# A hybrid decoder block: weights split a block ahead, dense banks kept open, recurrence inputs moved

## The chip, the cores and the metric

The kernel runs on one core of one Trainium2 chip. The metric is device time in microseconds, the median of three runs. The core has a matrix engine (TensorE, PE in the profile; PEld is its weight load), and three engines for elementwise work: VectorE (DVE), ScalarE (ACT) and GpSimd (POOL). SyncE (SP) issues the DMAs of the weights. TensorE writes to PSUM, which has eight banks of 128 partitions by 512 float32 numbers; all other data lie in SBUF.

## The reference

One decoder layer over 512 positions of width 1024. The input is normalized and projected once (`xn @ w_in`), and the columns of the result go to four branches of width 512 and to their gates:

- A, forgetting attention, 8 heads of 64 with a cumulative log-sigmoid bias: `s = q.k * scale + c_i - c_k`, causal softmax, `o = p v`;
- B, a recurrence: a causal convolution of width 4 over `xb`, two sigmoid gates by block-diagonal matrices, then `h_t = a_t h_(t-1) + b_t`;
- C, sparse attention, 8 heads over 2 key heads, the gated sum of three attentions: over compressed blocks of 32 positions (a small MLP over 32 x 64 values with stride 16), over selected blocks (all of them here) and over a window;
- D, spatial gating: `gelu(ud)` times a causal mix of the layer-normed `gelu(vd)`.

Each branch is multiplied by the SiLU of its gate (`ga`, `gb`, `gc`, `gd`), projected to 1024 columns, weighted by `sigmoid(mg)` and summed; `out = x + merged @ w_out`.

## The kernel before

Every product is made from three float32r matmuls: each operand is split into a rounded high part and the rest, and high x high, low x high and high x low are summed in PSUM. So each weight block of 128 x 1024 is loaded (`load`, a 512 KB DMA into one of four `raw` buffers), cast to its high part on POOL or ACT (`hi_cast`) and subtracted on DVE (`wsplit`, three `w` buffers).

The projections are written as generators. `zgen` makes one bank (128 columns of the result, transposed, by 512 positions) in 8 steps of three matmuls of 512 columns. `nat` makes four banks (512 positions by 512 columns) from four weight blocks in 32 steps. A list `queue` holds such generators, and `fill(us)` runs steps from it, at an assumed `G` = 0.68 us a step, between the parts of an attention. `drain` empties it. These generators ask for the weight block when their turn comes, and `nat` takes its four banks at its start.

The attentions go by units, one head of one kind each. `scores` makes four score tiles (L503, L504), their masked maximum (L506, DVE) and exponential (L508, ACT), and calls `fill` after each. POOL scales the probabilities (L516). `finish` transposes them in pieces of 128 x 256 (L527), splits each piece (ACT L532, DVE L533), multiplies by the values (L540, L541), and calls `fill` between. `attend` runs `scores` of a unit ahead of `finish` of the one before.

The program order is:

1. `ka`, `qa`, `va` and the norm of x.
2. Attention A, 8 units, with a queue of `kv`, `qc`, `cm` (the inputs of the compression) and `vd`. Then `drain`, and `psum_banks` closes all PSUM pools and opens others.
3. Attention C, 16 units. `compress()` writes shifted copies of `cm` (`t2`, `trs`, L701 to L707), splits them (`tbl`, L709, L712), and runs the MLP (`hps`, L723) and makes the compressed keys `kc`. It runs beside the `ga` blocks (`both`), and the second unit waits for it in the program (`while not ready`). `ud`, `gd` and two blocks of `gc` are queued behind. Then `drain`, and `psum_banks` again.
4. The late stage: `xb` blocks, whose use copies each bank to SBUF (L960) and convolves it on DVE (L962, L966), the rest of `gc`, the gates (L979 to L983), gelus, the recurrence's scan, `gb`, and the first merge of branch A (`merge_plain`: `mg` blocks, then `project`). Then the spatial mix and the sums that the next stage needs.
5. Three merges by seven block products each (`seven`, `project`), and the output projection.

The program order is not the engines' order. The framework's planner simulates the program when it is built: it gives each engine the earliest written instruction that is ready by its own estimates, so that later work moves into gaps, as far as buffers and banks are free. A pool's memory that follows a closed pool is free when the old tiles have been read. Each engine then runs its list in that order, waiting where an operand is late.

Of the kernel before, what the change touches and what calls it, by code (L numbers as in the profile page):

```python
# [1 line left out]

# [58 lines left out]
def f32(ap):  # L61
    return ap.bitcast(F32)
# [3 lines left out]
def tile_hybrid_layer(ctx: ExitStack, tc: tile.TileContext, x, xT, units, small, bsp, out):  # L66
# [10 lines left out]
    def psum_banks(nz, nt, rest):  # L77

        if "stack" in ps_:
            ps_["stack"].close()  # L80
        ps_["stack"] = st = ExitStack()
        ps_["n"] += 1
        ps_.pop("m", None)
        ps_["nz"] = nz
        for nm in ("z", *rest):
            ps_[nm] = pool(f"{nm}p{ps_['n']}", st, space=PSUM)
        ps_["tb"] = [ps_["t"].tile([P, S], F32, name=f"tb{i}") for i in range(nt)] if nt else []
        ps_["ti"] = 0
# [4 lines left out]
    def four(name):  # L93

        if "m" in ps_:
            return [zbank(name + "0")] + [ps_["m"].tile([P, S], F32, tag="m", bufs=3, name=f"{name}{t}") for t in (1, 2, 3)]
        return [zbank(f"{name}{t}") for t in range(4)]
# [10 lines left out]
    psum_banks(4, 1, "sto")  # L108
# [61 lines left out]
    G = 0.68  # L170
    last = {}

    def zgen(key, b, use):

        hi, lo = wsplit(key, b)
        ps = zbank(f"z_{key}{b}")
        for k in range(KD):
            ks = slice(k * P, (k + 1) * P)
            PE.matmul(ps, lhsT=hi[:, ks], rhs=xh[:, k, :], start=k == 0, stop=False)  # L179
            PE.matmul(ps, lhsT=hi[:, ks], rhs=xl[:, k, :], start=False, stop=False)  # L180
            PE.matmul(ps, lhsT=lo[:, ks], rhs=xh[:, k, :], start=False, stop=k == KD - 1)  # L181
            if k == KD - 1:
                use(ps)
            yield G

    def nat(key, lhs_h, lhs_l, emit, fetch=None):

        banks = four(f"z_{key}")
        for c in range(4):
            hi, lo = (fetch or wsplit)(f"{key}.{c // 2}", c % 2)  # L190
            for t in range(4):
# [11 lines left out]
    queue, owed = [], [0.0]  # L203

    def fill(us):

        owed[0] += us
        while owed[0] > 0 and queue:
            c = next(queue[0], None)
            if c is None:  # L210
                queue.pop(0)
            else:
                owed[0] -= c
        owed[0] = min(owed[0], 0.0)

    def drain():
        while queue:
            fill(1.0)

    def both(a, b):  # L220

        live = [a, b]
        while live:
            c = 0.0
            for g_ in list(live):
                d = next(g_, None)
                if d is None:
                    live.remove(g_)
                else:
                    c += d  # L230
            if c:
                yield c
# [11 lines left out]
    def run(gen, n=10 ** 6):  # L244
        for _ in range(n):
            if next(gen, None) is None:
                return

# [193 lines left out]

    att = ExitStack()
# [158 lines left out]
    def cm_use(b):  # L602
        return lambda ps: ACT.copy(zcm[b], ps)
# [13 lines left out]
    for e, o in ((0, 64), (1, 0)):  # L617
        POOL.tensor_scalar(kts[1][1][o:o + 40, e, :], f32(nb), 1.0, 0.0, op0=ALU.mult, op1=ALU.add)
    queue += [nat("kv", xh, xl, emit_kv), nat("qc", xh, xl, emit_z(zq_c, ssc, 4, 8, ap)),
              zgen("cm0", 0, cm_use(0)), zgen("cm0", 1, cm_use(1)), nat("vd", xh, xl, emit_vd)]  # L620

    def fox_units():
        for i in range(4):
# [14 lines left out]
    def attend(units):  # L638
        prev = None
        for u in units:  # L640
            scores(u, G)
            if prev:
                finish(prev, GAPS)
            prev = u
        fill(6 * G)
        finish(prev, GAPS)

    attend(fox_units())
    drain()
    r1.close()  # L650
    psum_banks(3, 2, "sto")

    dp_ = pool("dp_", side="right")
    def tile8(name, dtype=F32):
        return dp_.tile([P, 4, S], dtype, tag="t8", bufs=2, name=name)

    r2 = ExitStack()
    rp2 = pool("rp2", r2, side="right")
# [15 lines left out]
    def silu(key, dst, blocks=(0, 1, 2, 3), keep=False):  # L674
        for i in blocks:
            yield from zgen(f"{key}{i // 2}", i % 2, silu_use(dst, i, key, keep))
# [10 lines left out]
    def compress():  # L687
# [7 lines left out]
        trs = rp2.tile([P, 2048], F32, name="trs")  # L695

        def prepare(n, nm):
# [3 lines left out]
            POOL.memset(tr[:, :, :, 31:32], 0.0)  # L701
            for g in range(2):
                t2 = ap.tile([P, S], F32, tag="ft", bufs=3, name=f"t2{nm}{g}")
                ACT.copy(t2[0:64, :], zcm[n][HALF[g], :])
                ACT.copy(t2[64:128, 0:511], zcm[n][HALF[g], 1:512])
                src = bass.AP(tensor=t2.tensor, offset=t2.offset, ap=[list(t2.ap[0]), [2, 16], [16, 31]])
                DVE.tensor_tensor(tr[:, :, g, 0:31], src, cc[:, POS:POS + 16].unsqueeze(2).to_broadcast([P, 16, 31]),  # L707
                                  op=ALU.add)
# [8 lines left out]
        def hidden(nm):  # L717
            hps = zbank("hps" + nm)[:, 0:256]
            for h in range(2):
                w = wsplit("w1" + nm, h, True)  # L720
# [39 lines left out]
        for c in prepare(1, "v"):  # L760
            yield c + next(gk)
# [82 lines left out]
    def gd_():  # L844
        sgd["t"] = ylp.tile([P, 4, S], F32, tag="z8", bufs=1, name="sgd")
        yield from silu("gd", sgd["t"], keep=True)

    queue.append(gd_())
# [3 lines left out]
    fill(4 * G)  # L852

# [34 lines left out]
    attend(nsa_units())  # L888
# [52 lines left out]
    psum_banks(3, 0, "mg")  # L941
# [15 lines left out]
    def xb_use(i):  # L957
        def use(ps):
            xb = lp.tile([P, S], F32, tag="xb", bufs=2, name=f"xb{i}")
            ACT.copy(xb, ps)  # L960
            xc[i] = ft(f"xc{i}", "xc", 4)
            DVE.tensor_scalar(xc[i], xb, cc[:, CONVW + 12 + i:CONVW + 13 + i], cc[:, CONVB + i:CONVB + i + 1],  # L962
                              op0=ALU.mult, op1=ALU.add)
            for k in (2, 1, 0):
                n = 3 - k
                DVE.scalar_tensor_tensor(xc[i][:, n:], xb[:, 0:S - n], cc[:, CONVW + 4 * k + i:CONVW + 4 * k + i + 1],  # L966
                                         xc[i][:, n:], op0=ALU.mult, op1=ALU.add)
            xch = lp.tile([P, S], F32R, tag="xch", bufs=2, name=f"xch{i}")
            xcl = lp.tile([P, S], F32R, tag="xcl", bufs=2, name=f"xcl{i}")
            POOL.tensor_scalar(xch, xc[i], 1.0, 0.0, op0=ALU.mult, op1=ALU.add)  # L970
            DVE.tensor_tensor(xcl, xc[i], f32(xch), op=ALU.subtract)
            xsp[i] = (xch, xcl)
        return use
# [100 lines left out]
    queue.append(merge_plain(0, y["a"]))  # L1074
    lru_scan()
    queue.append(silu("gb", y["b"]))
    fill(40 * G)
    late.close()
    cnt["act"] = 3
# [185 lines left out]
    psum_banks(8, 0, "")  # L1265
# [73 lines left out]
    ps_["stack"].close()  # L1339
# [83 lines left out]
```

## Time and profile before

| | |
|---|---|
| median of 3 runs | 761.72 us (761.6 to 762.8) |
| profiled execution | 761.57 us |
| its span, first to last instruction | 758.6 us |
| TensorE busy | 725.1 us (96%) |
| VectorE busy | 553.6 us (73%) |
| ScalarE busy | 345.0 us (45%) |
| GpSimd busy | 191.1 us (25%) |
| mean granted TensorE clock | 0.991 |

Busy time is the union of an engine's instructions. A matmul's record is longer than the time between two matmuls, so a busy TensorE need not be at its peak. Times of the stretches below are microseconds from the start of the span.

### The profile page before, as it was taken

To read this page: it belongs to the slowest core of one execution; us is meant where nothing else is said; L and a number is where in the kernel's file an instruction comes from. 1 tells how busy PE (TensorE), PEld (TensorE's weight loads), DVE (VectorE), ACT (ScalarE), POOL (GpSimd) and SP (SyncE) were. 2 spreads that over 40 slices of the span, in tenths; PEclk is the share of its full clock that TensorE was granted. 3 is DMA by queue.
4 is the path that set the end of the run, shared out by engine and by line. 5 is a ranking of instruction groups with operands and counts; after the bars stand their busy time and mean duration, and the time that the engine had idled before them with its cause. 6 is when DMAs were issued, how large, how long until landed. Compare 5 with 4: busy or idle time off the path is not lost.

```text
span 758.6 us, 9587 instructions
## 1 busy us (share of the span) xinstructions
PE 725.1 (96%) x3387; PEld 579.4 (76%) x3387; DVE 553.6 (73%) x1025; ACT 345.0 (45%) x705; POOL 191.1 (25%) x245
## 2 busy tenths in 40 slices
PE   8999999998897999999998999999999999999998
PEld 6878777776665677877775787888788888888886
DVE  5698757676577865778877979979958957966622
ACT  4422655563663454565662672213551652563310
POOL 5153644346344023142334322510000000000000
PEclk9999999999998999999999999999999999999999
DMA  8613311212102411101001123243343143153031
GB/s 308 216 56 105 112 55 57 70 44 82 57 29 81 142 55 57 56 29 56 29 29 56 56 93 116 84 139 130 130 156 113 45 145 117 59 164 111 0 111 55
DMA packets 20495, 68.34 MB, mean 90 GB/s; under 512 B 2400, under 2 KB 2528, under 8 KB 20448
## 3 DMA queue, kind: packets, MB, share of 16 engines
q1 hardware_dynamic: 19008, 65.28, 25.3%
q10 hardware_dynamic: 1440, 2.46, 1.0%
q8 instruction: 26, 0.43, 0.2%
q14 instruction: 21, 0.17, 0.1%
HBM read 65.64 MB, written 2.10 MB: 89 GB/s over the span
## 4 chain that ended last, share of the span: by engine, by line
PE 45%; DVE 10%; ACT 3%; issue 2%; POOL 2%; POOLq 0%; ACTq 0%
PE pj L935 3%; PE pj L934 3%; PE pj L933 3%; PE out L1303 2%; PE out L1302 2%; PE out L1304 2%; PE tb L527 1%; PE o_s L541 1%; PE z_mg L196 1%; PE z_mg L197 1%; PE z_mg L198 1%; PE o_s L540 1%; PE z_gd L179 1%; PE z_gd L181 1%; PE z_gd L180 1%
## 5 line engine op out<-in xcount | busy, mean ns | idle before, releaser
L933 PE MATMUL pj<-w_wb,yh 128*128 128x512 f32 x128 | 50.1, 391 | 1.3 <-ACT tm L905 1.3
L934 PE MATMUL pj<-w_wb,yl 128*128 128x512 f32 x128 | 49.9, 390 | 0.0
L935 PE MATMUL pj<-w_wb,yh 128*128 128x512 f32 x128 | 49.9, 390 | 0.0
L516 POOL TENSOR_SCALAR p_w<-p_w,nm_w 128x128 f32<-128x128 f32 (+3 forms) x32 | 17.1, 552 | 51.4 <-DVE nm_w L513 27.7
L532 ACT CAST ph_a<-tb 128x256 fp32r<-128x256 f32 x40 | 14.8, 371 | 33.0 <-PE tb L527 30.7
L167 DVE TENSOR_TENSOR w_wb<-r_wb,w_wb 128x1024 fp32r<-128x1024 f32 x16 | 20.8, 1301 | 12.4 <-ACT w_wb L151 12.4
L933 PEld LDWEIGHTS pj<-w_wb,yh 128*128 128x128 f32 x128 | 24.0, 188 | 7.1 <-ACT tm L905 2.1
L935 PEld LDWEIGHTS pj<-w_wb,yh 128*128 128x128 f32 x128 | 24.0, 188 | 5.0
L934 PEld LDWEIGHTS pj<-w_wb,yl 128*128 128x128 f32 x128 | 24.0, 188 | 5.0
L533 DVE TENSOR_TENSOR pl_a<-tb,ph_a 128x256 fp32r<-128x256 f32 x40 | 16.8, 421 | 14.4 <-ACT ph_a L532 14.0
L516 POOL TENSOR_SCALAR p_s<-p_s,nm_s 128x128 f32<-128x128 f32 (+3 forms) x32 | 19.5, 628 | 30.6 <-ACT ph_w L532 19.1
L1312 DVE TENSOR_TENSOR xr<-out,xr 128x512 f32<-128x512 f32 x8 | 5.5, 692 | 27.1 <-PE out L1304 27.1
L508 ACT ACTIVATE p_s<-p_s,nm_s 128x512 f32<-128x512 f32 (+3 forms) x32 | 17.8, 559 | 11.7 <-DVE nm_s L506 11.1
L532 ACT CAST ph_w<-tb 128x256 fp32r<-128x256 f32 x40 | 14.0, 371 | 16.0 <-PE tb L527 15.6
L533 DVE TENSOR_TENSOR pl_w<-tb,ph_w 128x256 fp32r<-128x256 f32 x40 | 15.9, 419 | 6.5 <-ACT ph_w L532 6.3
L516 POOL TENSOR_SCALAR p_a<-p_a,nm_a 128x128 f32<-128x128 f32 (+3 forms) x32 | 18.4, 593 | 8.6 <-DVE nm_a L511 7.0
L508 ACT ACTIVATE p_w<-p_w,nm_w 128x512 f32<-128x512 f32 (+3 forms) x32 | 17.8, 558 | 4.7 <-DVE nm_w L506 4.5
L532 ACT CAST ph_s<-tb 128x256 fp32r<-128x256 f32 x40 | 14.0, 372 | 13.0 <-PE tb L527 12.8
L533 DVE TENSOR_TENSOR pl_s<-tb,ph_s 128x256 fp32r<-128x256 f32 x40 | 16.2, 418 | 5.0 <-ACT ph_s L532 4.6
L506 DVE CUSTOM_DVE_ANT_0 p_s<-s_s,maskm 128x512 f32<-128x512 f32 (+3 forms) x32 | 15.1, 488 | 6.3 <-PE s_s L504 4.8
L508 ACT ACTIVATE p_a<-p_a,nm_a 128x512 f32<-128x512 f32 (+3 forms) x32 | 17.7, 555 | 4.0 <-DVE nm_a L506 3.9
L151 ACT CAST w_wb<-r_wb 128x1024 fp32r<-128x1024 f32 x12 | 12.6, 1046 | 13.4 <-PE pj L935 10.8
(909 smaller groups left out, 2519.5 us busy)
## 6 DMA issues: line engine op xcount, KB each, us to landing
r_wb<-in_units_dram SPq DMA_DIRECT2D x16, 512.0 KB, 3.5
xt<-in_x_dram SPq DMA_DIRECT2D x4, 512.0 KB, 7.7
r_ga<-in_units_dram SPq DMA_DIRECT2D x4, 512.0 KB, 3.5
r_ud<-in_units_dram SPq DMA_DIRECT2D x4, 512.0 KB, 3.5
r_gd<-in_units_dram SPq DMA_DIRECT2D x4, 512.0 KB, 5.1
r_gc<-in_units_dram SPq DMA_DIRECT2D x4, 512.0 KB, 3.5
r_xb<-in_units_dram SPq DMA_DIRECT2D x4, 512.0 KB, 3.5
r_gb<-in_units_dram SPq DMA_DIRECT2D x4, 512.0 KB, 3.5
```

What stands on the lines that cost most here:

```text
L167: DVE.tensor_tensor(w[:, 1, :], raw, f32(w[:, 0, :]), op=ALU.subtract)
L506: DVE.tensor_tensor_reduce(out=pi, in0=s[:, :n], in1=maskm[:, 384 - i * P:512], scale=-1.0, scalar=BIG, op0=ALU.add, op1=ALU.min, accum_ou ...
L508: ACT.activation(pi, pi, AF.Exp, scale=-1.0, bias=nm[:, i:i + 1], accum_out=nm[:, 4 + i:5 + i])
L516: POOL.tensor_scalar(pi, pi, nm[:, 8 + i:9 + i], 0.0, op0=ALU.mult, op1=ALU.add)
L532: ACT.copy(ph[:, c:c + 256], t_)
L533: DVE.tensor_tensor(pl_[:, c:c + 256], t_, f32(ph[:, c:c + 256]), op=ALU.subtract)
L933: PE.matmul(banks[t], lhsT=yh[:, k, ts_], rhs=hi[:, cs], start=k == 0, stop=False)
L934: PE.matmul(banks[t], lhsT=yl[:, k, ts_], rhs=hi[:, cs], start=False, stop=False)
L935: PE.matmul(banks[t], lhsT=yh[:, k, ts_], rhs=lo[:, cs], start=False, stop=k == 3)
L1302: PE.matmul(pos, lhsT=mh[:, k, ts_], rhs=hi[:, ws], start=k == 0, stop=False)
L1303: PE.matmul(pos, lhsT=ml[:, k, ts_], rhs=hi[:, ws], start=False, stop=False)
L1304: PE.matmul(pos, lhsT=mh[:, k, ts_], rhs=lo[:, ws], start=False, stop=k == KD - 1)
```

## The change

- **PSUM.** The pools are opened and closed one by one. `z` has three banks, at the other end of PSUM, and stays open from the start through both attentions to the last stage. A fourth bank for `nat` blocks is a pool `x` during attention A; after `vd` it is closed and becomes the second transposing bank `t2`. The late stage closes `t2`, `t`, `s`, `o` and opens `m`, `g`.
- **Weights a block ahead.** A generator yields `AHEAD` once its weight block is loaded and split. `step` calls the next generator in the queue for its split after three steps of the present one. `nat` becomes four `chunks`, queued one by one.
- **Side work.** `both` goes. Generators in `side` advance once with each dense step: the shifted copies (`spread`, put there by the second `cm` block, in attention A) and `compress`, that begins with the splits of both inputs and has its own buffer for the MLP weights.
- **Pace.** `attend` has a factor on the fills in `scores` and `finish`: 1.2 in attention A, 1.1 in attention C.
- **Queue.** Two `ga` blocks are queued ahead of the last head of A; the queue is not emptied after A, only `vd` is finished. Behind it come the other `ga` blocks, `gd`, `ud`, two `gc` blocks, and the four `xb` blocks, whose use is only the copy, into a pool of their own below the attention's. The convolution is a function in the late stage, with its high cast on ACT instead of POOL; the first merge is queued ahead of it.

```diff
-    psum_banks(4, 1, "sto")
+    ps_["nz"], ps_["ti"] = 3, 0
+    psum_open("z")
+    psum_open("s", "o")
+    psum_open("t")
+    psum_open("x")
...
     def zgen(key, b, use):
         hi, lo = wsplit(key, b)
+        yield AHEAD
         ps = zbank(f"z_{key}{b}")
...
+    def step():
+        c = queue[0].next()
+        if c is None:
+            queue.pop(0)
+            return 0.0
+        if queue[0].steps == 3 and len(queue) > 1 and not queue[1].ready:
+            c += queue[1].next() or 0.0
+        if c:
+            for g in list(side):
+                d = next(g, None)
...
     def cm_use(b):
-        return lambda ps: ACT.copy(zcm[b], ps)
+        def use(ps):
+            ACT.copy(zcm[b], ps)
+            if b == 1:
+                side.append(chain(spread(0, "k"), spread(1, "v")))
...
+                if h == 7:
+                    later(*silu("ga", y["a"], range(2)))
...
-    attend(fox_units())
-    drain()
+    attend(fox_units(), FOX)
+    while any(d.gen in vds for d in queue):
+        step()
     r1.close()
-    psum_banks(3, 2, "sto")
+    psum_close("x")
+    psum_open("t2")
...
-        for _ in range(12):
+        for _ in range(4):
             yield 0.0
         yield from prepare(0, "k")
+        yield from prepare(1, "v")
...
-    queue.append(both(silu("ga", y["a"]), compress()))
-    queue += [zgen(f"ud{i // 2}", i % 2, ud_use(i)) for i in range(4)]
...
+    side.append(compress())
+    later(*silu("ga", y["a"], range(2, 4)), *(zgen(f"gd{i // 2}", i % 2, gd_use(i)) for i in range(4)),
+          *(zgen(f"ud{i // 2}", i % 2, ud_use(i)) for i in range(4)))
...
-                queue.append(silu("gc", y["c"], (0, 2)))
+                later(*silu("gc", y["c"], (0, 2)), *(zgen(f"xb{i // 2}", i % 2, xb_use(i)) for i in range(4)))
...
-    queue += [zgen(f"xb{i // 2}", i % 2, xb_use(i)) for i in range(4)]
-    queue.append(silu("gc", y["c"], (1, 3)))
-    fill(20 * G)
+    later(*silu("gc", y["c"], (1, 3)), merge_plain(0, y["a"]))
     for i in range(4):
-        lru_gates(i)
-        fill(8 * G)
+        conv(i)
+        fill(3 * G)
+        if i:
+            lru_gates(i - 1)
+            fill(3 * G)
```

## Rows read from the trace of the kernel before

**Rows 1.** The page, part 1: busy us, share of the span, instructions.

```profile
PE 725.1 (96%) x3387; PEld 579.4 (76%) x3387; DVE 553.6 (73%) x1025; ACT 345.0 (45%) x705; POOL 191.1 (25%) x245
```

**Rows 2.** Windows: start:end and length, busy us of each engine, granted clock, DMA.

```profile
80.00:199.00 119.00, 112.77 (x546) 86.78 (x545) 79.38 (x201) 64.94 (x161) 55.62 (x70) 1.00 0.21 71
216.50:258.20 41.70, 34.10 (x157) 25.62 (x155) 33.81 (x72) 22.15 (x54) 15.13 (x17) 0.92 0.27 89
258.20:385.70 127.50, 123.64 (x669) 98.62 (x668) 95.96 (x285) 73.01 (x213) 37.39 (x61) 1.00 0.14 46
385.70:404.40 18.70, 16.16 (x87) 11.80 (x86) 13.27 (x35) 9.72 (x32) 8.72 (x14) 1.00 0.13 44
404.40:549.40 145.00, 140.97 (x626) 114.53 (x626) 130.49 (x171) 60.75 (x85) 31.97 (x25) 0.99 0.30 102
610.00:640.00 30.00, 30.00 (x134) 24.86 (x133) 21.17 (x23) 12.82 (x16) 0.00 (x0) 1.00 0.37 124
```

**Rows 3.** Windows of L180 alone, the second matmul of each `zgen` step.

```profile
201.00:216.50 15.50, 5.32 (x13) 2.46 (x13) 1.00 0.21 68
216.50:258.20 41.70, 12.53 (x29) 6.03 (x29) 0.92 0.27 89
258.20:385.70 127.50, 35.22 (x87) 16.52 (x87) 1.00 0.14 46
```

**Rows 4.** Timeline, 201 to 202: start us, us, instruction [idle before, releaser].

```profile
201.03 0.59 ACT L608 COPY vd<-z_vd 128x512 f32<-128x512 f32 x1
...
201.67 0.50 PE L179 MATMUL z_ga<-xh,w_ga 128*128 128x512 f32 x1 [1.89 <-ACT vd L608]
```

**Rows 5.** Timeline, 226 to 236.

```profile
226.93 1.98 DVE L712 TENSOR_TENSOR tblk<-trs,tblk 128x1024 fp32r<-128x1024 f32 x1
...
228.96 0.74 PE L723 MATMUL hpsk<-w_w1k,tblk 128*128 128x256 f32 x4 [2.45 <-DVE tblk L712]
...
234.43 1.20 DVE L167 TENSOR_TENSOR w_ga<-r_ga,w_ga 128x1024 fp32r<-128x1024 f32 x1
...
235.67 0.79 PE L181 MATMUL z_ga<-xh,w_ga 128*128 128x512 f32 x1 [2.79 <-DVE w_ga L167]
```

**Rows 6.** Tile `trs`: duration ns min/median/max, first and last start us.

```profile
L707 DVE TENSOR_TENSOR trs<-t2k,cc x2: 1001/1016/1030, 222.3 to 224.2; 128x496 f32<-128x496 f32 x2
```

**Rows 7.** The page, part 6: a DMA issue, KB, us to landing.

```profile
r_xb<-in_units_dram SPq DMA_DIRECT2D x4, 512.0 KB, 3.5
```

**Rows 8.** Tile `z_xb`, and the timeline at 405.6.

```profile
L179 PE MATMUL z_xb<-xh,w_xb x32: 389/397/796, 351.1 to 411.9; 128*128 128x512 f32 x32
...
L960 ACT COPY xb<-z_xb x4: 585/588/592, 405.0 to 413.1; 128x512 f32<-128x512 f32 x4
...
405.64 0.80 PE L179 MATMUL z_xb<-xh,w_xb 128*128 128x512 f32 x1 [1.28 <-ACT xb L960]
```

**Rows 9.** Tile `xch`, and groups by line of DVE, 404.4 to 549.4.

```profile
L970 POOL TENSOR_SCALAR xch<-xc x4: 616/617/958, 414.5 to 422.2; 128x512 fp32r<-128x512 f32 x4
L971 DVE TENSOR_TENSOR xcl<-xc,xch x4: 679/1100/1526, 415.2 to 424.4; 128x512 fp32r<-128x512 f32 x4
...
L914 DVE TENSOR_TENSOR yl<-y_a,yh 128x512 fp32r<-128x512 f32 x4 | 2.7, 688 | 0.1
```

**Rows 10.** The chain of waits, 519 to 549.6, its first and last piece on DVE.

```profile
519.89 0.47 DVE mx L1057
...
548.74 0.62 DVE mg2z L1196
```

**Rows 11.** Timeline of PE: the first scores of units 2 and 16 of attention C.

```profile
258.23 0.48 PE L503 MATMUL s_w<-ka_w,q_c 128*128 128x512 f32 x1
...
385.69 0.45 PE L503 MATMUL s_w<-ka_w,q_c 128*128 128x512 f32 x1
```

More of the change, by code (lines that the diff above doesn't have):

```diff
@@ L1 @@
 from contextlib import ExitStack, nullcontext
+from itertools import chain
 import concourse.bass as bass
@@ L75, in tile_hybrid_layer, with psum_open, psum_close @@
     ps_ = {"n": 0}
[L77 to L88, printed above, removed]
+    def psum_open(*names):
+        st = ExitStack()
+        for nm in names:
+            ps_["n"] += 1
+            ps_[nm] = pool(f"{nm}p{ps_['n']}", st, space=PSUM, **({"side": "right"} if nm == "z" else {}))
+        ps_[names] = st
+    def psum_close(*names):
+        ps_.pop(names).close()
+        for nm in names:
+            del ps_[nm]
     def zbank(name):
@@ L170, in tile_hybrid_layer @@
     G = 0.68
+    AHEAD = object()
     last = {}
@@ L184, in zgen, with chunks, chunk @@
             yield G
-    def nat(key, lhs_h, lhs_l, emit, fetch=None):
-        banks = four(f"z_{key}")
-        for c in range(4):
+    def chunks(key, lhs_h, lhs_l, emit, fetch=None):
+        banks = []
+        def chunk(c):
             hi, lo = (fetch or wsplit)(f"{key}.{c // 2}", c % 2)
+            yield AHEAD
+            if c == 0:
+                banks[:] = four(f"z_{key}")
             for t in range(4):
@@ L201, in nat, with __init__, next, later @@
                     yield G
-    queue, owed = [], [0.0]
+        return [chunk(c) for c in range(4)]
+    def nat(*args):
+        for c in chunks(*args):
+            yield from c
+    class Dense:
+        def __init__(self, gen):
+            self.gen, self.ready, self.steps = gen, False, 0
+        def next(self):
+            c = next(self.gen, None)
+            if c is AHEAD:
+                self.ready = True
+                return 0.0
+            self.steps += c is not None
+            return c
+    queue, owed, side = [], [0.0], []
+    def later(*gens):
+        queue.extend(Dense(g) for g in gens)
+    def step():
+        c = queue[0].next()
+        if c is None:
+            queue.pop(0)
+            return 0.0
+        if queue[0].steps == 3 and len(queue) > 1 and not queue[1].ready:
[3 more added lines that the diff above has]
+                d = next(g, None)
+                if d is None:
+                    side.remove(g)
+                else:
+                    c += d
+        return c
     def fill(us):
@@ L208, in fill, with drain, settle @@
         while owed[0] > 0 and queue:
[L209 to L213, printed above, removed]
-        owed[0] = min(owed[0], 0.0)
[L216 to L232, printed above, removed]
+            owed[0] -= step()
+        owed[0] = min(owed[0], 0.0)
+    def drain(n=0):
+        while len(queue) > n:
+            step()
+    def settle():
+        n = len(queue)
+        if queue and queue[0].steps:
+            drain(n - 1)
     def rsqrt(v, y, t):
@@ L244, in run @@
     def run(gen, n=10 ** 6):
-        for _ in range(n):
-            if next(gen, None) is None:
+        while n:
+            c = next(gen, None)
+            if c is None:
                 return
+            n -= c is not AHEAD
     xh = xp.tile([P, KD, S], F32R, tag="xh", bufs=1, name="xh")
@@ L674, in silu, with attend, tile8 @@
     def silu(key, dst, blocks=(0, 1, 2, 3), keep=False):
-        for i in blocks:
-            yield from zgen(f"{key}{i // 2}", i % 2, silu_use(dst, i, key, keep))
+        return [zgen(f"{key}{i // 2}", i % 2, silu_use(dst, i, key, keep)) for i in blocks]
+    def attend(units, pace=1.0):
+        gaps = [pace * g for g in GAPS]
+        prev = None
+        for u in units:
+            scores(u, pace * G)
+            if prev:
+                finish(prev, gaps)
+            prev = u
+        fill(6 * G)
+        finish(prev, gaps)
+    NSA = 1.1
+    FOX = 1.2
+    attend(fox_units(), FOX)
+    while any(d.gen in vds for d in queue):
+        step()
+    r1.close()
+    psum_close("x")
+    psum_open("t2")
+    ps_["tb"].append(ps_["t2"].tile([P, S], F32, name="tb1"))
+    dp_ = pool("dp_", side="right")
+    def tile8(name, dtype=F32):
+        return dp_.tile([P, 4, S], dtype, tag="t8", bufs=2, name=name)
+    r2 = ExitStack()
+    rp2 = pool("rp2", r2, side="right")
     kc = [rp2.tile([P, 2, 32], F32R, name=f"kc{g}") for g in range(2)]
@@ L852, in tile_hybrid_layer, with xb_use @@
     fill(4 * G)
+    def xb_use(i):
+        return lambda ps: ACT.copy(xbt[:, i, :], ps)
     def add_cmp(cell, e):
```

127 lines of the change are left out of this document (69 added, 58 removed).

## The prediction

> **What bounds the kernel now.** I read the page's busy table first: TensorE is busy for 725.1 of 758.6 us, VectorE for 553.6 [rows 1]. The reader is to see that TensorE can gain 33.5 us of idle time at most, and that nothing in the change removes matmuls. The table by stretches comes next [rows 2]. In 610 to 640 TensorE is never idle: 134 matmuls in 30.00 us, 0.224 us each, so one dense step (three matmuls, "step" below) is 0.67 us. The stretches before differ. From 216.5 to 258.2, between the two attentions, 7.6 of 41.7 us are idle and the granted clock is 0.92, which is one sixth of the stretch at 1.2 instead of 2.4 GHz, some 3.3 us of lost work. From 258.2 to 385.7 the idle time is 3.9 of 127.5 us, from 385.7 to 404.4 it is 2.5 of 18.7, from 404.4 to 549.4 it is 4.0 of 145.0. After 549.4 I expect no difference.
>
> The timeline says what the idle time is. At 199.8 TensorE waits 1.89 us for the copy of the last `vd` bank before `ga` may use it [rows 4]; that is the emptied queue and the reopened banks. At 226.5 it waits 2.45 us for `tblk`, whose subtraction on VectorE ended late, and at 232.9 it waits 2.79 us for the subtraction of a `ga` weight [rows 5]; the lower clock follows. At 404.4 it waits 1.28 us because the banks are full of `xb` results that may be copied only when the attention's SBUF is released [rows 8]. The chain of waits, last, says who is behind it: from 519.89 to 549.4 it runs nearly without a break over VectorE, 29 us of it, and in 404.4 to 549.4 VectorE is busy for 130.5 of 145.0 us [rows 2, 10]. So the kernel has two limits in turn: TensorE with its waits until 404, VectorE within about a tenth behind it from there to 549.
>
> The span is 758.6 us and the profiled execution took 761.57, so 2.97 us lie around the span. The median is 761.72, 0.15 above; I forecast from the profiled execution.
>
> **The change part by part.** I count dense steps. Up to the last write of the first attention (216.5) the kernel runs 112 queued steps (four blocks of 32, 32, 16 and 32) and already 20 of `ga`, since 13 full sets of the second matmul lie in 201 to 216.5 and the planner rearranges freely [rows 3]; I take 18 as done, 130 in all. The changed kernel has 256 steps to place before the second attention ends: those 112, `ga` 32, `gd` 32, `ud` 32, half of `gc` 16, and the moved `xb` 32.
>
> *First attention, to 216.5.* The bank wait of 1.89 us [rows 4] goes, because the dense banks stay open and `ga` is queued before the last head; what is late next is the same TensorE queue, so I count all of it. Pace 1.2 puts a fifth more dense steps between dependent ones; TensorE idles 6.2 of 119 us there [rows 2]. I take a quarter of that, 1.6 us, with bounds of 3 us worse (three instead of four rotating banks for `cm`) and 4 us better. The shifted copies come in here: two additions of 1.0 us on VectorE for each of the two inputs, 4.0 in all [rows 6], and eight short copies on ScalarE. VectorE is busy for 79.4 and ScalarE for 64.9 of 119 us here [rows 2], so they are hidden by TensorE's dense steps; uncovered they would cost 4 us. The attention's tiles lie 8 KB higher, above the `xb` pool, and so behind other early tiles; no row prices that, and the 3 us worse holds it. End of this stretch: 213.0.
>
> *Weights one block ahead.* Every load of 512 KB lands 3.5 us after its issue [rows 7], and a cast and subtraction follow. They are the same instructions, emitted five steps (3.4 us) earlier and so ahead of softmax work on VectorE. SP's queue issues earlier, behind the same four raw buffers; POOL's casts come ahead of POOL's scaling of the probabilities, on which the transposes wait. What it takes away is the 2.79 us at 232.9 [rows 5]; bounds 0 and 2.8 gained, and up to 2.8 lost where a softmax instruction now waits behind a subtraction. Its value is within the next sum.
>
> *Between the attentions.* Compression runs beside the dense steps and needs about 71 of them from where the first attention's program ends, of which about 14 of `ga` already lie before 213, some 55 after it. Before, 29 steps lie in 216.5 to 258.2 [rows 3], 19.4 us; with 7.6 idle and 3.3 of clock that leaves 11.4 us of other TensorE work. After: 55 steps are 36.9 us, the same 11.4, and a loss that I put at 4 us (bounds 1.1, the rate of the next stretch, and 10.9, nothing gained). So the second score block, that waits for the compressed keys, starts at 213.0 + 52.3 = 265, 7 us later than at 258.2, with more dense work done.
>
> *Second attention.* The scores of unit 2 start at 258.23 and those of unit 16 at 385.69 [rows 11]: 14 intervals with 87 steps [rows 3]. 127.5 - 87 x 0.67 = 69.2, 4.94 us an interval beside the dense steps. After, 256 - 130 - 57 = 69 steps remain, 46.2 us: 265.3 + 46.2 + 69.2 = 380.7, and the same 18.7 us for the end [rows 2] makes 399.4. Behind these the planner can bring forward steps of the other half of `gc` and the first merge, some 22 (three banks), 0 to 14.7 us; as gaps take part of them I add 5: 404.4, exactly where it ends now, but with 8 steps of `xb` and up to 22 more done. The `xb` copies themselves (4 x 0.588 us on ScalarE [rows 8]) move under this attention, where ScalarE has half its time free.
>
> *After it, to 549.4.* TensorE has 5.4 us of `xb` less here and up to 14.7 us of the rest: 141.0 busy falls to 121 to 136. VectorE's 130.5 us stay: convolution, gates, scan, splits are all still emitted here. Gone are perhaps two weight subtractions of 1.2 us, and 1.6 us at the moved cast: four `xcl` subtractions take 1.10 us in the median where four like ones, `yl`, take 0.69 [rows 9]; two ran at 0.68 and the slow ones lie beside POOL's work. So VectorE's floor is 126.5, and with half of its present 14.5 us of waits it is 134, with the present ones 141. The first merge is now queued ahead of the convolution, so its eight weight subtractions compete with the chain of gates and scan, while TensorE has other work; nothing is added by that. I take 137.0, 8.0 us less than 145.0; the floor would give 18.5, and where a gap on TensorE lets the clock fall again, 0.
>
> On those `xcl` the Trainium skill, SBUF — State Buffer, section "SBUF: two separate sides", says that a VectorE operation with two SBUF inputs and a GpSimd operation exclude each other for the whole instruction. By that rule the `bd` and `mg` casts that stay on POOL would go on lengthening them, and the gain of 1.6 us would be nearer 0.8.
>
> Sum: 0.0 at 404.4 (gains of 3.5 and 6.9 before it, spent on the moved steps) and -8.0 behind: span 750.6, time 753.6. I round to 753.5.
>
> **The rivals.**
> *Nothing much changes.* The planner already brings `xb` forward by 50 us, from 351.1 to before 404 [rows 8], so an earlier place in the program need not move an instruction; the waits at 226 and 232 are VectorE running later than planned, and these can recur. Then only the bank wait goes, 1.9 us, and VectorE holds the rest: 760. Against it: the copies that compression waits for really leave the stretch.
> *TensorE stays the limit throughout.* The Trainium skill, Perfetto Trace Analysis, "Identifying the Most-Contended Engine", says to optimize the engine of highest occupancy first, and by busy time that is TensorE. As a mechanism of this kernel: the whole idle and clock loss of 216.5 to 258.2 goes down to 1.1 (9.8 gained), the bank wait gives 1.9, pace 4, the wait at 404 1.3, the clock behind it 1.4 (0.99 of 145 us), a quarter of the 6.4 us idle in the second attention 1.6; that is 20.0, VectorE follows near its floor, and the time is 741.5. Against it stand the 29 us of VectorE in the chain [rows 10].
> *Slower: dense work runs out in the second attention.* The place is its last seven units. 71 steps are spent ahead of the second unit's turn, and what is left is emitted at 10 steps a unit, so after about seven units only work brought forward remains. Where an interval without dense steps costs 7.0 us instead of 4.94 (scores, exponentials, transposes and two copies in a row), seven of them cost 14.4 us more: the attention ends at 413.8 less what fits into the gaps for nothing (the 5 us): 408.8 to 413.8. With VectorE unable to return more than 3 us: 404.4 + 9.4 - 3 gives +6.4, 768. It decides from 6.1 us an interval on, where 7 x 1.2 eats the 8 us. For it: VectorE and ScalarE are a serial chain in a unit. Against it: the last intervals now hold few steps and keep the same 4.9 us rate.
>
> **How the numbers follow.** My forecast, 747 to 758, has 0.42; TensorE limit (below 747) 0.16; little change (758 to 763.2) 0.20; slower 0.22. A difference of 0.2% (1.5 us, 760.2 to 763.2) is about what can be told from no change here. Faster: 0.42 + 0.16 + half of 0.20 = 0.68; same 0.10; slower 0.22. The range leaves out 0.07 below 741 and 0.11 above 768; the forecast's own is 747 to 758.
>
> **What would show it.** Right: no wait for the `vd` copy ahead of `ga`; compression's first matmul without a wait for `tblk`; clock 1.00 between the attentions; `xb` copies under the second attention; last value matmul of it at 404 +- 6; from there to the end of the second merge's first part about 137 us with VectorE over 92% busy. Wrong: TensorE idle more than 6 us in the second half of the second attention, new stretches at the lower clock behind it, or a VectorE that shrinks below 126 us there.

## The result, and the profile after

The changed kernel takes 752.18 us in the median of four runs (750.47 to 753.83), the kernel before 761.66 in runs beside it: ratio 0.9878, 95% interval 0.9846 to 0.9910. The profiled execution took 753.83 us, 751.9 of them the span, which is 6.7 less than before. A second set of runs of the same kernel measured 752.39 us and the ratio 0.9886 (0.9868 to 0.9904).

The page, part 1, answers to [rows 1]:

```profile
PE 723.0 (96%) x3387; PEld 579.9 (77%) x3387; DVE 552.0 (73%) x1025; ACT 347.7 (46%) x710; POOL 198.3 (26%) x240
```

TensorE's idle time went from 33.5 to 28.9 us, its busy time by 2.1: the same 3387 matmuls ran with fewer gaps. VectorE has lost 1.6 us of work. Which stretch gave it is in the windows, cut at the same events as in [rows 2] (start:end and length; busy us of PE, PEld, DVE, ACT, POOL; granted clock; DMA share; GB/s):

```profile
80.00:199.00 119.00, 110.90 (x525) 84.91 (x524) 83.21 (x196) 67.62 (x164) 53.95 (x73) 0.99 0.20 68
219.80:279.10 59.30, 56.53 (x265) 45.21 (x264) 39.98 (x80) 20.88 (x51) 20.68 (x16) 0.97 0.32 107
279.10:392.80 113.70, 112.19 (x618) 89.24 (x617) 87.47 (x277) 73.12 (x215) 36.79 (x59) 1.00 0.13 43
392.80:408.40 15.60, 15.23 (x85) 11.82 (x85) 10.49 (x33) 9.02 (x28) 6.22 (x9) 1.00 0.11 35
408.40:542.80 134.40, 125.79 (x564) 102.59 (x562) 128.33 (x169) 60.50 (x85) 36.66 (x23) 0.99 0.31 103
```

The dense steps in them, by the second matmul of each, answer to [rows 3] (busy us of PE and PEld):

```profile
219.80:279.10 59.30, 26.61 (x66) 12.75 (x66) 0.97 0.32 107
279.10:408.40 129.30, 31.15 (x77) 14.77 (x78) 1.00 0.12 42
408.40:542.80 134.40, 13.72 (x35) 6.47 (x35) 0.99 0.31 103
```

The reader is to take each stretch less 0.67 us for each of its dense steps (in the first row these are counted by all matmuls on the `z` banks from 80 us on); what remains is the time that TensorE spent on everything else and on waiting. Before, 94 steps lay in the whole second attention and 56 behind it; `mg` steps and projections behind it are the same in both.

| stretch | before: length, steps, remainder | after | remainder's change |
|---|---|---|---|
| 80 to the first attention's end | 136.5, 126, 52.1 | 139.8, 128, 54.0 | +2.0 |
| between the attentions | 41.7, 29, 22.3 | 59.3, 66, 15.1 | -7.2 |
| second attention | 146.2, 94, 83.2 | 129.3, 77, 77.7 | -5.5 |
| behind it, to the second merge | 145.0, 56, 107.5 | 134.4, 35, 111.0 | +3.5 |

The four changes add up to -7.2 us, which is what the stretch between the attentions gained by itself. The last two rows belong together, since steps moved from one to the other: their remainders are 190.7 us before and 188.7 after. The late stage is 10.6 us shorter because 21 of its steps (14.1 us of TensorE's time) had been done before. That its remainder grew by 3.5 us doesn't say that it became worse: VectorE is busy there for 128.3 of 134.4 us, so a step taken out of it need not shorten it by 0.67 us.

### The profile page after: what moved, and what is told of

It reads as the page before. It is cut to its first block, busy times and chain, and to the rows that moved or that the text cites. A ratio compares the mean times of both kernels' runs of the same rounds, so it can differ in the third digit from the quotient of the medians.

```text
span 751.9 us, 9588 instructions
## 1 busy us (share of the span) xinstructions
PE 723.0 (96%) x3387; PEld 579.9 (77%) x3387; DVE 552.0 (73%) x1025; ACT 347.7 (46%) x710; POOL 198.3 (26%) x240
## 4 chain that ended last, share of the span: by engine, by line
PE 66%; DVE 18%; ACT 8%; issue 4%; POOL 2%; DMA 1%; SPq 0%; POOLq 0%; DVEq 0%; ACTq 0%
PE tb L573 3%; PE pj L1014 3%; PE pj L1015 3%; PE pj L1016 3%; PE out L1389 2%; PE out L1390 2%; PE out L1391 2%; PE o_s L587 1%; PE o_s L586 1%; PE z_gd L191 1%; PE z_ka L212 1%; PE z_ka L210 1%; PE z_gd L189 1%; PE z_gd L190 1%; PE z_ka L211 1%
## 5 line engine op out<-in xcount | busy, mean ns | idle before, releaser
L562 POOL TENSOR_SCALAR p_w<-p_w,nm_w 128x128 f32<-128x128 f32 (+3 forms) x32 | 20.2, 649 | 37.4 <-DVE nm_w L559 15.7
L578 ACT CAST ph_s<-tb 128x256 fp32r<-128x256 f32 x40 | 14.2, 371 | 14.0 <-PE tb L573 13.7
L573 PE MATMUL tb<-identf,p_a 128*128 128x128 f32 x80 | 16.6, 288 | 3.2 <-DVE q_a L505 1.1
L578 ACT CAST ph_w<-tb 128x256 fp32r<-128x256 f32 x40 | 14.1, 371 | 10.7 <-PE tb L573 10.2
```

What stands on the lines that cost most here:

```text
L562: POOL.tensor_scalar(pi, pi, nm[:, 8 + i:9 + i], 0.0, op0=ALU.mult, op1=ALU.add)
L573: PE.transpose(t_[:, c * P:(c + 1) * P], u.p[:, OFF[i] + j * P:OFF[i] + (j + 1) * P], identf)
L578: ACT.copy(ph[:, c:c + 256], t_)
```

## The experiments

Every ratio is to the kernel before, run beside it, with its 95% interval.

**The same kernel again.**

> The changed kernel again, as the yardstick for the runs beside it. Both theories: 750 to 754 us, 0.985 to 0.991 of the kernel before.

752.39 us, 0.9886 (0.9868 to 0.9904). Its profile has a span of 748.9 us, 3.0 under the first one, and 3.4 us at the lower clock level where the first has 10.2 (behind the first 20 us and ahead of the last 5). Between the attentions its remainder is 13.7 us where the first has 15.1. Differences of 3 us between two profiles are therefore not read as effects below.

**Moves undone one at a time.** `xb` back in the late stage of the program, its pool left where it is:

```diff
-  later(*silu("gc", y["c"], (0, 2)), *(zgen(f"xb{i // 2}", ...) for i in range(4)))
+  later(*silu("gc", y["c"], (0, 2)))
...
+  later(*(zgen(f"xb{i // 2}", ...) for i in range(4)), *silu("gc", y["c"], (1, 3)), merge_plain(0, y["a"]))
```

> The recurrence inputs are queued in the late stage again, with copy and convolution in one use, but the copy still goes to the pool below the attention's. Theory A (a place to copy to is what counts, the planner brings the matmuls forward by itself): first xb matmul before 390, copies before the second attention ends, time 752 to 755 us. Theory B (the place in the program counts): xb matmuls after 400, time 757 to 761 us.

761.73 us, 1.0003 (0.9985 to 1.0021): the whole gain gone. Yet the planner brings the `xb` matmuls forward by itself, as theory A said: they start at 332 us, and the copies run from 347 to 397, under an attention that ends at 403. No look-ahead:

```diff
-        if queue[0].steps == 3 and len(queue) > 1 and not queue[1].ready:
-            c += queue[1].next() or 0.0
```

> No look-ahead: each block's load, cast and subtraction are written at its own turn. Theory A (look-ahead is worth what TensorE waited for weights, 2.8 us in one place, and the planner brings splits forward anyway): 751 to 755 us. Theory B (the splits a block ahead are the main gain): 757 us or more, with waits of TensorE for weight subtractions above 4 us in sum.

764.27 us, 1.0044 (1.0030 to 1.0058). Both misses looked like proof that these two moves are the gain. The waits of TensorE and the loads of `r_gb` say otherwise. Without look-ahead (waits: engine, line, releaser, us, times, longest):

```profile
PE z_gb L189 <- ACT w_gb L159: 8.1, 1, 8.1
```

```profile
512.32 0.33 SPq L1170 DMA_DIRECT2D r_mg21.00_4773<-in_units_dram  x1
512.70 0.43 SPq L1170 DMA_DIRECT2D r_mg21.01_4775<-in_units_dram  x1
513.17 0.43 SPq L1170 DMA_DIRECT2D r_mg21.10_4777<-in_units_dram  x1
513.64 0.47 SPq L1170 DMA_DIRECT2D r_mg21.11_4779<-in_units_dram  x1
519.63 0.33 SPq L165 DMA_DIRECT2D r_gb<-in_units_dram  x1
```

That is the timeline of SyncE's queue. The fourth `gb` weight is issued at 519.63, behind eight loads of the second merge, four of which are held until 512; with `xb` late it is issued at 514.8 and TensorE waits 6.1 us. In the changed kernel all four are out by 479:

```profile
L165 SPq DMA_DIRECT2D r_gb<-in_units_dram x4: 327/328/328, 464.5 to 478.9; - x4
```

The edits had shifted by a few steps what the queue held where the program passes the second merge's loads. If that order is the loss, emptying the queue there must give it back:

```diff
+    drain()
     cnt["act"] = 1
     head = blocks(2)
```

> The changed kernel, with the rest of the gb blocks written ahead of the loads of the second merge's weights instead of behind them. A control: in the changed kernel the fourth gb load is already issued first (478.9 against 489.6 us). Theory C (only the order of these loads matters) and its rival: 750 to 754 us.

> xb queued in the late stage as before, and the gb blocks written ahead of the second merge's loads. Theory C (the 9 us lost with xb late were the fourth gb load, issued behind eight loads of the second merge; the place of xb itself is worth nothing): no wait for the gb cast, 750 to 754 us. Theory B (xb's place in the program is worth it): 757 to 761 us.

> No look-ahead, and the gb blocks written ahead of the second merge's loads. Theory C (the 12 us lost without look-ahead were the fourth gb load): 752 to 755 us. Theory B (splits a block ahead are worth it throughout): 758 us or more.

Alone 753.15 us, 0.9899 (0.9878 to 0.9920); with `xb` late 752.7, 0.9889 (0.9867 to 0.9911); without look-ahead 750.83, 0.9879 (0.9854 to 0.9904). All three are at the changed kernel's ratio. So the loss of 9 and 12 us was the load order, and with that order kept neither the place of `xb` in the program nor the look-ahead moves the time measurably.

**The pool of the `xb` copies.** To the late `xb` and the emptied queue, the pool moves to the late stage:

```diff
-    xbt = pool("xbp", xbs).tile([P, 4, S], F32, name="xb")
+    xbt = None
...
     lp = pool("lp", late)
+    xbt = lp.tile([P, 4, S], F32, name="xb")
```

> Base: the kernel with `xb` queued in the late stage and the queue emptied ahead of the second merge's loads, which measured 752.7 us. Here the pool of the `xb` copies moves as well: it opens with the late stage, in memory that the attention has held, as before the change, so no copy can run until the attention ends and its banks stay full. Theory (the saving comes from where the copies may go): the `xb` results wait with full banks at the attention's end, a wait of 1 to 2 us on TensorE near 404, about 20 to 24 of the 32 steps run behind it, and most of the saving goes: 757 to 761 us. Rival (VectorE alone sets the end, TensorE's steps move freely): 751 to 754 us, with VectorE busy over 94% from the attention's end to the second merge.

754.24 us, 0.9912 (0.9888 to 0.9936): most of the gain stays, the time lies between the two ranges, and against 0.9889 with the pool below, the intervals overlap. Its windows between, in and behind the second attention, then the last two of the kernel that it starts from:

```profile
218.10:277.60 59.50, 56.73 (x266) 45.32 (x264) 40.03 (x80) 20.91 (x51) 20.68 (x16) 0.97 0.33 107
277.60:401.70 124.10, 116.96 (x637) 91.30 (x635) 95.88 (x307) 79.04 (x237) 44.30 (x72) 0.99 0.11 35
401.70:543.20 141.50, 138.53 (x628) 113.66 (x627) 129.92 (x171) 65.25 (x91) 28.84 (x20) 1.00 0.33 106
```

```profile
280.10:404.70 124.60, 121.19 (x670) 95.27 (x669) 97.37 (x308) 80.98 (x241) 41.99 (x68) 1.00 0.12 39
404.70:545.10 140.40, 134.67 (x595) 109.76 (x594) 127.97 (x170) 60.30 (x85) 32.03 (x24) 0.98 0.31 103
```

The copies wait for the attention again (402.3 to 408.8), and TensorE waits 1.3 us for one of them, as the theory said; but only 8 of the 32 `xb` steps lie behind, and VectorE is busy for 92% there, not 94%. TensorE stands idle for 7.1 us of the second attention instead of 3.4 in the kernel that it starts from and 1.9 in the changed one, and 56 steps lie behind it instead of 45 and 35. Against the first, 11 steps fewer make the attention 0.5 us shorter and 11 more make the late stage 1.1 us longer; against the second, 21 steps make 5.2 and 7.1 us, 0.25 and 0.34 us a step. These are single profiles with different clocks in them. In either comparison a step moved is worth about half of its 0.67 us or less in both stages, which fits moving steps bringing so little.

**The preparation of the compression.** Shifted copies back at the start of `compress`:

```diff
-            if b == 1:
-                side.append(chain(spread(0, "k"), spread(1, "v")))
...
+        for _ in chain(spread(0, "k"), spread(1, "v")):
+            pass
```

> The shifted copies and their additions are written at the start of the compression again, behind the first attention; everything else as changed. Theory A (dense steps hide them wherever they stand): 751 to 754 us. Theory B (their removal from between the attentions is the gain there): the wait of the first compression matmul for its operand returns, 2 us or more, and with it the lower clock; 755 to 759 us.

754.45 us, 0.9920 (0.9903 to 0.9937), between the two ranges and some 2 us over the changed kernel, whose interval it just touches (0.9868 to 0.9904). The same 66 steps lie between the attentions, in 62.4 us, with a new wait there, not the one that theory B named:

```profile
PE z_ga L189 <- DVE th_ga L717: 3.1, 1, 3.1
```

TensorE waits for a dense bank that VectorE reads late, at 226.6 us, behind the copies' additions (219.0 to 225.5). In the first attention, from 80 us to its end, TensorE is idle for 6.7 us instead of 8.7 (9.2 in the second profile of the changed kernel), so dense steps seem not to hide the copies wholly there.

**The pace.** Both factors at 1:

```diff
-    NSA = 1.1
-    FOX = 1.2
+    NSA = 1.0
+    FOX = 1.0
```

> The changed kernel with both paces at 1.0 instead of 1.2 and 1.1; nothing else. Theory (the paces only shift dense steps between stages, VectorE's stage takes what is left): the first attention ends some 3 us earlier than at 219.8 and fewer steps lie in it, the second ends within 3 us of 408, total 751 to 754 us. Rival (the pace is what keeps TensorE busy in the attentions): idle time returns in 80 to 199 and in the second attention, total 755 to 759 us.

760.47 us, 0.9993 (0.9980 to 1.0006). The rival's side but above its range, and the largest loss that the load order doesn't explain (the fourth `gb` load is out at 486.4, ahead of the first of the eight at 497.1); but not where the rival put it. Windows of this kernel, of all work and of the second matmul of each step:

```profile
80.00:199.00 119.00, 112.74 (x545) 86.34 (x544) 80.78 (x202) 66.09 (x163) 58.01 (x73) 1.00 0.22 71
219.70:281.80 62.10, 53.44 (x245) 41.95 (x243) 41.61 (x82) 20.55 (x50) 20.27 (x23) 0.92 0.29 95
281.80:415.60 133.80, 130.51 (x715) 104.76 (x716) 98.49 (x310) 81.98 (x242) 41.88 (x68) 1.00 0.13 43
```

```profile
219.70:281.80 62.10, 23.61 (x59) 11.19 (x59) 0.92 0.29 95
281.80:415.60 133.80, 33.40 (x83) 15.74 (x83) 1.00 0.13 43
```

In 80 to 199 TensorE is idle for 6.3 us, less than with the pace (8.1). Between the attentions it is idle for 8.7 instead of 2.8, at a clock of 0.92 instead of 0.97, and the remainder is 62.1 - 59 x 0.67 = 22.6: the 22.3 of before. The second attention has six more steps to do and ends 7.2 us later. The waits that it has there (TensorE, 219.7 to 281.8; the changed kernel has none of them):

```profile
PE tb L497 <- DVE kb_w L520: 3.5, 2, 1.9
PE hpsk L799 <- DVE w_w1k L792: 2.8, 2, 1.7
PE s_s L549 <- DVE q_c L505: 1.2, 1, 1.2
```

The first is a transposing bank that VectorE reads when it makes the key operand `kb_w`, the second a weight of the compression, the third a query. An obvious suspect is the shifted copies, first with the pace at 1, then in the changed kernel (ns min/median/max, first and last start):

```profile
L685 DVE TENSOR_TENSOR trs<-t2v,cc x2: 1009/1018/1026, 204.0 to 211.8; 128x496 f32<-128x496 f32 x2
```

```profile
L685 DVE TENSOR_TENSOR trs<-t2v,cc x2: 984/1006/1029, 183.1 to 184.6; 128x496 f32<-128x496 f32 x2
```

They advance with dense steps, and with fewer of these per unit they come 21 to 27 us later. But that isn't the 8 us: with the copies put back to 219 and later the loss was 2, and what is made of them, the subtraction of `tblk`, starts at 223.6 us here and at 223.1 in the changed kernel. The cause shows in TensorE's own list, from the end of the first attention to the first score of the second (busy us of PE; all its instructions, then those of the `ga` blocks), in the changed kernel and with the pace at 1:

```profile
219.80:231.95 12.15, 12.15 (x58) 1.00 0.01 2
219.80:231.95 12.15, 12.00 (x48) 1.00 0.01 2
```

```profile
219.70:232.58 12.88, 7.50 (x34) 0.83 0.14 42
219.70:232.58 12.88, 5.92 (x23) 0.83 0.14 42
```

That score starts 12.2 and 12.9 us behind the first attention, so VectorE has its keys and queries ready after nearly the same time. What differs is what TensorE does meanwhile: 48 matmuls of `ga` blocks and no wait, against 23 and 5.4 us of waits. The 25 fewer are 5.6 us at 0.224 each. They are not lacking: of the 96 `ga` matmuls 24 stand behind the score with the pace at 1, 6 in the changed kernel.

**Closed banks.** Queue emptied between the attentions, no `ga` ahead of the last head, dense banks closed and opened again:

```diff
-                if h == 7:
-                    later(*silu("ga", y["a"], range(2)))
...
-    while any(d.gen in vds for d in queue):
-        step()
+    drain()
     r1.close()
     psum_close("x")
+    psum_close("z")
+    psum_open("z")
```

> The changed kernel with the queue emptied between the attentions, no `ga` block ahead of the last head, and the dense banks closed and opened again there. Theory (the open banks matter): TensorE waits about 1.9 us for the last `vd` copy before `ga` as before the change, and the compression's waits stand open at the lower clock again, total 755 to 758 us. Rival (the emptied queue is filled from the other side by the planner, VectorE sets the end): the wait is there but total 752 to 754 us.

758.69 us, 0.9963 (0.9949 to 0.9977): 6 us of the gain go. The edit undoes three things at once, so it doesn't say which of them counts. The wait for the last `vd` copy is not among TensorE's waits there; most of the loss is between the attentions again, 60 steps in 59.2 us (remainder 19.0), and 5.1 us idle:

```profile
218.40:277.60 59.20, 54.13 (x250) 43.24 (x248) 39.70 (x79) 20.60 (x50) 19.70 (x18) 0.94 0.31 100
```

```profile
PE tb L497 <- DVE kb_w L520: 3.2, 2, 2.3
PE s_s L549 <- DVE q_c L505: 1.4, 1, 1.4
```

The waits are those of the pace at 1, though the shifted copies come as early as in the changed kernel (179.2 to 183.1 us). The rows from the end of the first attention to the first score tell the same as there, 12.5 us with 28 matmuls of `ga` blocks, and 24 behind:

```profile
218.40:230.92 12.52, 7.97 (x39) 0.96 0.01 2
218.40:230.92 12.52, 7.10 (x28) 0.96 0.01 2
```

**The late stage.** The changed kernel has a new wait there. Timeline of ScalarE, then of TensorE:

```profile
477.68 1.05 ACT L1179 CAST xs<-xs 128x1024 fp32r<-128x1024 f32 x1 [19.24 <-DVE xs L1215]
478.74 1.28 ACT L986 ACT_TABLE_LOAD   x1
480.03 2.06 ACT L986 ACTIVATE tm<-z_mg 128x512 f32<-128x512 f32 x4
```

```profile
481.17 0.80 PE L1014 MATMUL pj<-w_wb,yh 128*128 128x512 f32 x1 [4.53 <-ACT tm L986]
481.77 0.63 PE L1015 MATMUL pj<-w_wb,yl 128*128 128x512 f32 x1
```

ScalarE runs its list in order; the four tanh stand behind a cast for whose operand, made by VectorE, it is idle for 19.24 us; TensorE waits 4.53 us for them and goes on at the lower clock. With those casts on GpSimd:

```diff
-        ACT.copy(hi, src)
+        POOL.tensor_scalar(hi, src, 1.0, 0.0, op0=ALU.mult, op1=ALU.add)
```

> The changed kernel with the casts of the block sums for the second merge on GpSimd instead of ScalarE. Theory A (ScalarE stands 19 us in front of one such cast, whose operand VectorE makes late, and four tanh evictions stand behind it; TensorE waits 4.5 us for these and then runs 3.4 us at the lower clock): that wait goes, 745 to 749 us. Rival (VectorE's amount of work sets the end of this stage): 751 to 753 us.

754.69 us, 0.9911 (0.9890 to 0.9931), above both ranges. The wait for `tm` fell to 1.0 us, and the next one in line took its place:

```profile
PE sg L1132 <- POOL vnh L1117: 4.9, 1, 4.9
```

`vnh` is the cast of the normalized `vd`, which VectorE wrote only at 483 to 487. So VectorE's order seemed to be the limit, and the last kernel takes work from it, on the kernel without look-ahead: the convolution's first tap to ScalarE, `vnh` and the spatial weights' cast from GpSimd to ScalarE, the casts of the sums to GpSimd as above.

```diff
-        DVE.tensor_scalar(xc[i], xb, cc[...], cc[...], op0=ALU.mult, op1=ALU.add)
+        ACT.activation(xc[i], xb, AF.Identity, scale=cc[...], bias=cc[...])
...
-        POOL.tensor_scalar(wsh, wsr, 1.0, 0.0, op0=ALU.mult, op1=ALU.add)
+        ACT.copy(wsh, wsr)
...
-            POOL.tensor_scalar(vnh[:, t, :], v, 1.0, 0.0, op0=ALU.mult, op1=ALU.add)
+            ACT.copy(vnh[:, t, :], v)
```

> Base: the kernel without look-ahead and with the queue emptied ahead of the second merge's loads, which measured 750.8 us. Work beside or on VectorE moves away in the late stage: the convolution's first tap (4 x 0.54 us) to ScalarE, the casts of `vnh` and of the spatial weights from GpSimd to ScalarE (the subtractions behind them took 1.09 and 2.06 us where undisturbed ones took 0.68 and 1.21), and the casts of the summed inputs from ScalarE to GpSimd, behind which `tm` stood. Theory (VectorE sets the late stage): VectorE's busy time from the attention's end to the second merge falls from 128.6 by 4 to 5 us, and the time by as much: 745.5 to 748 us. Rival (the order on ScalarE and TensorE sets it): the new ScalarE work lies in front of tanh and sigmoid, the time stays within 749 to 753 us with a VectorE share under 93%.

752.88 us, 0.9884 (0.9861 to 0.9907): no gain, the rival. VectorE's busy time behind the attention fell from 128.4 to 125.6 us of 135.6, and the wait is now

```profile
PE sg L1130 <- ACT vnh L1115: 6.2, 1, 6.2
```

The 2.7 us that VectorE was given, less than the 4 to 5 expected, did not shorten the chain sums, statistics, `vd`, `vnh`. What stays shown is that one wait of 4.5 to 6.2 us stands at that place in each of the three orders; that VectorE's total is the limit is not shown. No kernel here is measurably faster than the changed one.

## Why the prediction was right, point by point

The time, 753.5, came within 1.4 us of the median, and the likeliest case held. Its steps did less well than its sum, which is right in part by luck.

*First attention, to 216.5: wrong.* It was put at 213.0 and ended at 219.8 in this profile (217 to 222 in the others). The term mis-sized is the gain of the open banks and the pace (1.9 and 1.6 us). The wait for the `vd` copy did go, but waits on VectorE's key and query work grew in its place, from 2.2 us (`kb_a` 1.5, `q_a` 0.7) to 5.4:

```profile
PE tb L497 <- DVE kb_a L520: 2.3, 4, 1.2
PE s_a L549 <- DVE q_a L505: 2.0, 3, 1.0
PE tb L573 <- DVE q_a L505: 1.1, 1, 1.1
```

Idle time is 8.1 of 119 us in 80 to 199, against 6.2 [rows 2]; the pace at 1 has 6.3 there and still ends at 219.7, with three more steps done, counted as above. From 80 us to the attention's end the remainder is 52.1 us before, 54.0 and 53.2 in the two profiles of the changed kernel, 53.6 without look-ahead and 53.0 with the pool of `xb` in the late stage again: neither of these two moves it beyond what two profiles of one program differ by. The copies, put at nothing, took some 2 us, if the one profile without them there is read so. The three banks are in every run, so their part stays open.

*Weights one block ahead: right that it is small.* With the load order kept, its removal measured nothing. Nor did it take the wait for a weight away: TensorE waits 2.1 us at 236 for a `gd` weight's subtraction (`z_gd` on `w_gd`), in place of the 2.79 for `ga` [rows 5]; without look-ahead it waits 0.4 us for the same weight and 1.3 for a bank. What the prediction had not seen is that a shift of a few steps can put one load behind eight others, at 9 to 12 us.

*Between the attentions: the rate right, the count wrong.* Eleven more steps lie there than the 55 forecast, but length less steps was forecast at 52.3 - 36.9 = 15.4 and measured 15.1. The wait for `tblk` is gone as said. The clock is 0.97, not 1.00, behind the wait at 236; in the second profile, with the same wait, it is 1.00. That the copies leave the stretch was the prediction's reason why the waits should not recur; the runs show a weightier one, below.

*Second attention: the rate right.* 4.94 us an interval was forecast; 113.7 us with 70 steps and 14 intervals give 4.77. It ends 4.0 us later than before, not at the same time, and with 21 steps fewer left behind it, which lies within the 8 and up to 22 counted. (The forecast's sum takes 57 steps off for the stretch before, where 55 were put there; that is 1.3 us.) The rival of dense work running out did not come: TensorE is idle for 0.4 of the last 15.6 us (2.5 of 18.7 before), so the moved steps fill the last intervals.

*After it: -8.0 forecast, -10.6 measured.* VectorE's floor of 126.5 was nearly right (128.3), and its waits fell from 14.5 to 6.1 us instead of halving. The four `xcl` subtractions, 1.10 us in [rows 9], measure as forecast:

```profile
L1053 DVE TENSOR_TENSOR xcl<-xc,xch x4: 675/678/680, 418.0 to 427.4; 128x512 fp32r<-128x512 f32 x4
```

GpSimd stands idle while they run, but for the last 0.05 us: its casts lie at 418.88 to 420.26 and from 428.03 on, the subtractions at 418.0, 423.0 and 426.8 to 428.1. So the full 1.7 us came, not the half that was weighed against it, because the casts that stayed moved out of the way. Where one did not, the last `vnl` beside a `w_gb` cast (490.04 to 491.09), the subtraction took from 490.11 on 1.52 us against 0.68 for the quickest. This agrees with the Trainium skill, SBUF — State Buffer, section "SBUF: two separate sides", by which the two engines exclude each other there.

*The sum.* Nothing at 404 and -8.0 behind were forecast, +4.0 and -10.6 measured: -8.0 against -6.6 in this pair of profiles. Two errors cancelled: the first attention did not gain its 3.5 us, and more steps had left the late stage.

*The rivals.* "Nothing much changes" failed on its price, yet its reason was sound: the planner does move work by itself, and neither the place of `xb` nor its pool is the gain. "TensorE stays the limit" (741.5) failed on the first attention and on the late wait. By the Trainium skill, Perfetto Trace Analysis, section "Identifying the Most-Contended Engine", one would have gone on to TensorE as the engine of highest occupancy (96% by its matmuls; 77% by its weight loads, by which the page would judge TensorE's headroom; VectorE has 73%); in the late stage VectorE is the busier one (128.3 of 134.4 against 125.8), and there taking work from it gained nothing either.

*What the gain is.* The remainder between the attentions is 22.3 us before, 15.1 with the change, 22.6 without the pace, 19.0 with the closed banks, 18.2 with the copies put back (62.4 - 66 x 0.67), and the times follow it: 761.7, 752.2, 760.5, 758.7, 754.5. In the other profile of the changed kernel and in those of six variants that measured 750.8 to 754.7 us it is 13.7 to 15.4; the kernel with the copies put back lies within their times, so of its loss little can be told. The two kernels that lost by the load order have 15.1 and 15.4, so the losses are of two kinds. Behind the first attention it takes VectorE and TensorE some 12 us in turns to make the keys and queries of the second, and in the changed kernel TensorE has 48 dense matmuls to do in that time, with the pace at 1 it has 23, with the banks closed and the queue emptied 28. With the copies put back VectorE is late instead: the first score starts 20.5 us behind the first attention. The kernel before lost there by other waits, for `tblk` and for the `ga` weight [rows 5]. So the pace is needed, and so is what the kernel with the closed banks undoes, whose three parts aren't told apart; the two losses add up to more than the gain. That the dense matmuls stand there or not, and that these two times follow, is shown; why the planner puts fewer of them there at the lower pace, and which of the two paces does it, stays open.

## What to carry to other kernels

Subtract the movable work from each stretch before comparing two traces: stretches of different length were the same work in other places here, and where TensorE was the limit the remainder told where time was won; where VectorE was, it did not. When a wait on another engine returns, ask first what the waiting engine had to do meanwhile: the operands came after nearly the same time here, and the filling was gone. When an edit that should cost nothing undoes a whole gain, look at the order of the loads behind limited buffers before believing it; one control with that order fixed changed two verdicts. And a removed wait in an engine that works its list in order is worth only the distance to the next one, so look that up first.

## What the runs showed of the hardware

The lower clock level (1.2 of 2.4 GHz) was granted for 3.4 us from 238.4, behind the 2.1 us wait at 236, for 3.4 us from 480.7, at the end of the 4.5 us wait, and for 10.2 us from 520.5 around the 8.1 us wait without look-ahead. At 481.77 the next `pj` matmul starts 0.42 us later, at the full level 0.23. So a wait can cost more than its length. Not every wait did: in the first profile of the changed kernel the 2.2 us for `xch` at the start of the late stage has no lower clock behind it, while the kernel with the pace at 1 has the same wait and 3.4 us of it from 426.2. In the second profile of the changed kernel the same 2.13 us wait for `w_gd` has none behind it either. The two profiles of the same program, 3.0 us apart in span, have 10.2 and 3.4 us at that level.
